# Second mixer of a two-layer trunk: group norm and output projection on half the tokens at a time, in two lanes beside the chain

## The chip, the cores and the metric

One core of one Trainium2 chip. The metric is the device time of one execution in microseconds. A core has engines that run their own queues in order: PE (matrix products; its weight loads are listed as PEld), DVE (elementwise work), ACT (functions and copies), POOL, and SP, which issues nearly all transfers here.

## The reference, cut to what matters

Two layers run over 1104 tokens (16 learned + 1024 prompt tokens, and 64 of a second request), 1024 channels, in f32. The second layer's mixer is RWKV-7: a recurrence over time for each of 16 heads of 64 channels, then

```python
y = moveaxis(scan(step, S0, ...))                # per token and head
y = ((y - mean) * rsqrt(var + GN_EPS)) * ln_w + ln_b   # group norm per head
y = y + bonus                                    # sum(r*k*r_k) * v
y = (y * gate) @ w_o                             # output projection
h = h + y
```

The layer's feed-forward network follows. The kernel computes the recurrence in chunks of 64 tokens.

## The kernel before

`rwkv_a` makes the inputs of the recurrence and leaves them in DRAM: among them the bonus `BV` (stored at L1454) and the gate `GT` (L1156), each as 8 blocks of 128 channels by 1152 tokens. `rwkv_b` runs the recurrence. Channels lie on partitions and tokens along the rows of a tile.

The work is cut into six batches `i`, each a group `g` of 384 tokens (three groups; the first has 320 live tokens) and a half `hf` of the channels (four blocks `ff` of 128). Batch `i` is run in stage `i`, 0 to 5, by `chain`: six chunks of 64 tokens, one after the other, each a row of small matmuls (L1689, L1699, L1704, L1711, L1725) with short steps between them: copies `pm` (L1691), scaled copies (L1705 on ACT, L1706 on DVE), the new state `st` (L1713, L1717), and at the end of a chunk the copy `ysb` of its output (L1726). Beside the chain of batch `i` the stage prepares the next batches: `Bx.build` (tile products, with mask multiplies at L1557 and L1558 on DVE), `Bx.grams`, and `Bx.inverse`, whose start is a substitution of many small DVE operations (L602, L604), then DVE transposes (L618, L620), then small matmuls.

The finished batch `i-1` goes through `tail` in the same stage. First, for each `ff`, it loads `lbv` and `lgt`, squares `y`, sums it with a plain f32 matmul against `bd64` (L1746), takes the inverse root (L1748, L1749 on ACT), and scales, adds and gates on DVE (L1750 to L1752). `split` then makes a rounded part `yh` (ACT, L108) and a remainder `yl` (DVE, L109). Second, for four pairs `mp` of output blocks, `wunit` loads 512 KB of w_o (`raw`), splits it into `wh` (ACT) and `wl` (DVE), and `mm3` sends three products per channel block through PE (L129 to L131). The residual add (L1768, `xt`) follows. In groups 0 and 1 the residual row `xt` is loaded from DRAM and stored again.

What sets the order: each part is a generator, `weave` steps the generators of a stage in turn (each by its share of steps: the chain 36, `tail` 16), and then a scheduler of the framework orders each engine's instructions by that priority and by its own estimate of when inputs are ready. The orders below are what came out. A tile pool with `bufs` slots per tag makes a writer wait until the oldest slot is read; in stages 1 to 4 `raw` has two slots, `wh` and `wl` have one.

Of the kernel before, what the change touches and what calls it, by code (L numbers as in the profile page):

```python
# [51 lines left out]
def tile_trunk(ctx, tc, *aps, stages=("gdn", "ffn0", "rwkv", "ffn1"), dbg=None):  # L52
# [1077 lines left out]
    def gates(tp, xp, dr):  # L1130
# [52 lines left out]
    def rwkv_a(hnp, col, prm, pc, plb, dr, esb, esx, esg, pend, esP):  # L1183
        C = math.exp(-0.5)
        with ExitStack() as es0, ExitStack() as es:
# [246 lines left out]
            with ExitStack() as es, ExitStack() as es1:  # L1432
# [5 lines left out]
                def post_v(ps, n, g, f):  # L1438
# [182 lines left out]
    def rwkv_b(xT, rc, col, plb, dr, Bx, gts, esx, esg, esf, esh, F, more):  # L1621
# [9 lines left out]
        with ExitStack() as esw, ExitStack() as es, ExitStack() as est:  # L1631
# [97 lines left out]
            def tail(g, hf, B):  # L1729
# [5 lines left out]
                for ff in range(4):  # L1735
                    f = 4 * hf + ff
                    bv = tp.tile([P, 384], F32, tag="lbv", bufs=lb, name=uid("lbv"))
                    nc.sync.dma_start(bv[:, :n], dr["BV"][f, :, cs])
                    gt = tp.tile([P, 384], F32, tag="lgt", bufs=lb, name=uid("lgt"))
                    nc.sync.dma_start(gt[:, :n], dr["GT"][f, :, cs])  # L1740
                    y = B["y"][:, ff].rearrange("p c t -> p (c t)")[:, o:]
# [8 lines left out]
                    nc.vector.scalar_tensor_tensor(rs, y, col("rwkv_ln_w", f), rs, ALU.mult, ALU.mult)  # L1750
                    nc.vector.scalar_tensor_tensor(rs, rs, col("rwkv_ln_b", f), bv[:, :n], ALU.add, ALU.add)
                    nc.vector.tensor_tensor(rs, rs, gt[:, :n], ALU.mult)  # L1752
                    split(yy[0][:, ff, :n], yy[1][:, ff, :n], rs)
                    yield
                c0 = LIVE[g][0]
                for mp in range(4):
                    u = wunit(w_o[512 * hf:512 * hf + 512, 256 * mp:256 * mp + 256].rearrange("(k p) c -> p k c", p=P), *wpo)
                    wv = [t.rearrange("p (k m) c -> p k m c", m=2) for t in u]
                    for mm in range(2):
# [21 lines left out]
            tpt, wpo = [], []  # L1781
            ypool = (tp, 2)
            for i, (g, hf) in enumerate(seq):
                Bi = Bx.at(i)
                extra = []
                if i == 5:
# [11 lines left out]
                    if more:  # L1798
                        extra = [(FA, then(first(fp0, hp), F.std(range(N5), (0,), fp0, wunits, lambda i: psB()), F.norms(fp0, (1,))), FO)]
                gens = [(CH, then(chain(i, g, hf, Bi, 0), chain(i, g, hf, Bi, 1)))] + extra  # L1800
                if i == 0:
# [15 lines left out]
                done = tail(g, hf, Bi)  # L1817
            est.close()
# [124 lines left out]
    if "rwkv" in stages:  # L1943
        rs_ = {k: dp_.tile([8, P, 1152], F32, name="r" + k) for k in ("V", "GT", "BV", "R")}
        for k in ("KR", "BK"):
# [50 lines left out]
```

## Time and profile before

| | us |
|---|---|
| median of 3 runs | 3335.11 |
| lowest, highest | 3333.39, 3340.08 |
| the profiled execution | 3338.0 |
| its span | 3336.3 |
| stage 0 of the second mixer's chain ends | 2147.5 |
| stage 5 ends | 2536 |

Times inside the trace are microseconds from the span's start. A stage is taken to end with the sixth `ysb` copy (L1726, on ACT) of its batch, and a chunk with its own. "Busy" is time in which an engine has an instruction; on PE the ends are modelled, since matmuls overlap. The granted clock is the share of full TensorE speed.

### The profile page before, as it was taken

The page shows a single profiled execution, that of the slowest core. Times are in us where ns is not written, and L with a number is a line of the kernel's source. Part 1 is how long each engine was busy: PE and PEld are TensorE (multiplying, and loading weights), DVE is VectorE, ACT ScalarE, POOL GpSimd, SP SyncE. Part 2 cuts the span into 40 slices and gives each one's busy share as a digit, 9 for nine tenths or more (in the row PEclk, how much of TensorE's full clock was granted, in tenths as well). Part 3 has the DMA queues.
Part 4 walks back from the last instruction along what each step waited for, and adds up shares of the span by engine and source line. Part 5 has one row for each costly group of instructions (what it writes and reads, how often), then busy time and mean ns, then how long its engine had stood idle before and what let it go on. Part 6 is the DMA issues. An engine that isn't in the chain of part 4 may idle for free. (4 is left out here: it accounts for less than half of the span.)

```text
span 3336.3 us, 72764 instructions
## 1 busy us (share of the span) xinstructions
PE 3162.9 (95%) x29202; PEld 2974.1 (89%) x29202; DVE 2432.8 (73%) x4835; ACT 1562.6 (47%) x3141; POOL 142.1 (4%) x236
## 2 busy tenths in 40 slices
PE   7999999898999999999999888998989999999998
PEld 6888888797999999999988777777778999999998
DVE  6967768457777667776978863777767687877775
ACT  5876766444433333212777742544445443333112
POOL 1000000002200000000001100000000310000000
PEclk8999999999999999999999899998889999999999
DMA  5433332784332224432255877555556333335231
GB/s 161 120 105 102 100 92 71 268 304 132 99 104 81 79 72 159 130 106 76 78 183 168 278 222 241 148 165 168 152 172 186 100 104 91 94 97 174 88 96 61
DMA packets 543923, 452.69 MB, mean 136 GB/s; under 512 B 78377, under 2 KB 494930, under 8 KB 543458
## 3 DMA queue, kind: packets, MB, share of 16 engines
q1 hardware_dynamic: 538682, 445.61, 43.7%
q8 instruction: 230, 3.77, 0.5%
q10 hardware_dynamic: 4904, 2.43, 0.3%
q14 instruction: 107, 0.88, 0.1%
HBM read 306.86 MB, written 141.07 MB: 134 GB/s over the span
## 5 line engine op out<-in xcount | busy, mean ns | idle before, releaser
L310 PE MATMUL psA<-tc,sh 128*128 128x276 f32 (+1 forms) x1712 | 499.6, 292 | 18.8 <-ACT sh L108 8.2
L312 PE MATMUL psA<-tc,sl 128*128 128x276 f32 (+1 forms) x1712 | 498.9, 291 | 4.0 <-DVE sl L109 3.9
L311 PE MATMUL psA<-tc,sh 128*128 128x276 f32 (+1 forms) x1712 | 498.9, 291 | 0.3 <-DVE tc L109 0.3
L406 DVE TENSOR_TENSOR xT<-xT,psA 128x384 f32<-128x384 f32 (+3 forms) x496 | 252.3, 519 | 136.1 <-PE psA L131 134.4
L310 PEld LDWEIGHTS psA<-tc,sh 128*128 128x128 f32 x1712 | 326.2, 191 | 21.4 <-ACT sh L108 8.6
L108 ACT CAST wh<-raw 128x1024 fp32r<-128x1024 f32 x159 | 166.0, 1047 | 372.5 <-PE psA L130 258.6
L312 PEld LDWEIGHTS psA<-tc,sl 128*128 128x128 f32 x1712 | 325.7, 190 | 5.0 <-DVE sl L109 4.7
L311 PEld LDWEIGHTS psA<-tc,sh 128*128 128x128 f32 x1712 | 325.9, 190 | 1.2 <-DVE tc L109 0.7
L130 PE MATMUL psA<-hl,wh 128*128 128x384 f32 (+3 forms) x1024 | 326.4, 319 | 0.0
L129 PE MATMUL psA<-hh,wh 128*128 128x384 f32 (+3 forms) x1024 | 325.8, 320 | 0.0
L131 PE MATMUL psA<-hh,wl 128*128 128x384 f32 (+3 forms) x1024 | 325.3, 318 | 0.0
L129 PE MATMUL psA<-hnh,wh 128*128 128x384 f32 (+1 forms) x768 | 269.1, 350 | 5.1 <-ACT hnh L108 3.8
L130 PE MATMUL psA<-hnl,wh 128*128 128x384 f32 (+1 forms) x768 | 261.4, 340 | 1.7 <-DVE hnl L109 1.7
L131 PE MATMUL psA<-hnh,wl 128*128 128x384 f32 (+1 forms) x768 | 260.1, 339 | 0.0
L109 DVE TENSOR_TENSOR wl<-raw,wh 128x1024 fp32r<-128x1024 f32 x159 | 195.0, 1228 | 72.8 <-ACT wh L108 72.6
L108 ACT CAST sh<-raw 128x512 fp32r<-128x512 f32 x202 | 124.4, 619 | 251.6 <-PE psA L311 230.8
L129 PE MATMUL psA<-mxh,wh 128*128 128x384 f32 (+1 forms) x672 | 226.4, 348 | 8.3 <-ACT mxh L108 5.3
L130 PE MATMUL psA<-mxl,wh 128*128 128x384 f32 (+1 forms) x672 | 229.2, 343 | 3.6 <-DVE mxl L109 3.5
L131 PE MATMUL psA<-mxh,wl 128*128 128x384 f32 (+1 forms) x672 | 227.5, 340 | 0.3 <-DVE wl L109 0.2
L129 PEld LDWEIGHTS psA<-hh,wh 128*128 128x128 f32 x1024 | 192.0, 188 | 0.7 <-ACT hh L108 0.4
L130 PEld LDWEIGHTS psA<-hl,wh 128*128 128x128 f32 x1024 | 192.3, 188 | 0.3
L131 PEld LDWEIGHTS psA<-hh,wl 128*128 128x128 f32 x1024 | 192.5, 188 | 0.1
(482 smaller groups left out, 7958.8 us busy)
## 6 DMA issues: line engine op xcount, KB each, us to landing
raw<-in_ffn_w_gate_dram SPq DMA_DIRECT2D x64, 512.0 KB
raw<-in_ffn_w_up_dram SPq DMA_DIRECT2D x64, 512.0 KB
raw<-in_ffn_w_down_dram SPq DMA_DIRECT2D x44, 512.0 KB
raw<-in_gdn_w_in_dram SPq DMA_DIRECT2D x32, 512.0 KB
raw<-in_gdn_w_out_dram SPq DMA_DIRECT2D x24, 512.0 KB
raw<-in_rwkv_w_o_dram SPq DMA_DIRECT2D x24, 512.0 KB
hr<-dhid SPq DMA_DIRECT2D x44, 276.0 KB
hr<-dhid SPq DMA_DIRECT2D x44, 272.0 KB
```

Source lines behind the costliest of these rows:

```text
L108: nc.scalar.copy(h, src)
L109: (eng or nc.vector).tensor_tensor(l, src, h.bitcast(F32), ALU.subtract)
L129: nc.tensor.matmul(ps, w[0][:, k, :], x[0][:, k, :n], start=a, stop=False)
L130: nc.tensor.matmul(ps, w[0][:, k, :], x[1][:, k, :n], start=False, stop=False)
L131: nc.tensor.matmul(ps, w[1][:, k, :], x[0][:, k, :n], start=False, stop=z)
L310: nc.tensor.matmul(ps, u[0][:, kk], h, start=first and kk == 0, stop=False)
L311: nc.tensor.matmul(ps, u[0][:, kk], l, start=False, stop=False)
L312: nc.tensor.matmul(ps, u[1][:, kk], h, start=False, stop=last and kk == 3)
L406: nc.vector.tensor_tensor(xT[:, m, a:a + n], xT[:, m, a:a + n], pd[:, :n], ALU.add)
```

## The change

`BV` and `GT` are put into one DRAM tensor `BG`, so that one load `lbg` brings both. `tail` is kept for batches 4 and 5. For batches 0 to 3 it is replaced by two generators that each work on one half (192 columns) of a batch: `normed` (group norm) and `project` (w_o and residual add). The first half of the first group has 128 live columns.

- Stage `i` from 1 to 4 has a lane of `normed`: the second half of batch `i-1`, and (`i` below 4) the first half of batch `i` itself, as soon as `over` says that the chain's first three chunks are issued. Stage 1 begins with the first half of batch 0.
- Its other lane is `project` on batch `i-1`, first half, then second half. It yields until its half is in `ready`.
- `project` loads and splits all of w_o's part again for each half. Two output blocks share one PSUM tile, one residual load, one add and one store; the store is issued a step later (`late`).

The core of the diff:

```diff
-                    bv = tp.tile([P, 384], F32, tag="lbv", bufs=lb, name=uid("lbv"))
-                    nc.sync.dma_start(bv[:, :n], dr["BV"][f, :, cs])
-                    gt = tp.tile([P, 384], F32, tag="lgt", bufs=lb, name=uid("lgt"))
-                    nc.sync.dma_start(gt[:, :n], dr["GT"][f, :, cs])
+                    bg = tp.tile([P, 2, 384], F32, tag="lbg", bufs=lb, name=uid("lbg"))
+                    nc.sync.dma_start(bg[:, :, :n], dr["BG"][:, f, :, cs].rearrange("a p c -> p a c"))
...
+            def window(g, half):
+                o = 384 - LIVE[g][1]
+                lo = max(o, 192 * half)
+                return lo, 192 * half + 192 - lo, LIVE[g][0] + lo - o
...
+            def normed(i, half, out):
...
+                yy = [tp.tile([P, 4, 192], F32R, tag=t, bufs=2, name=uid(t)) for t in ("yh", "yl")]
+                for ff in range(4):
...
+                    ps = psC()
+                    nc.tensor.matmul(ps[:, :n], bd64, rs, start=True, stop=True)
+                    nc.scalar.activation(rs, ps[:, :n], AF.Ln, bias=gne)
+                    nc.scalar.activation(rs, rs, AF.Exp, scale=-0.5)
+                    nc.vector.scalar_tensor_tensor(rs, yf, col("rwkv_ln_w", f), rs, ALU.mult, ALU.mult)
+                    nc.vector.scalar_tensor_tensor(rs, rs, col("rwkv_ln_b", f), bg[:, 0, :n], ALU.add, ALU.add)
+                    nc.vector.tensor_tensor(rs, rs, bg[:, 1, :n], ALU.mult)
+                    split(yy[0][:, ff, :n], yy[1][:, ff, :n], rs)
+                    yield
+                out[i, half] = yy
...
+            def project(i, half, out):
+                while (i, half) not in out:
+                    yield
...
+                for mp in range(4):
+                    u = wunit(w_o[512 * hf:512 * hf + 512, 256 * mp:256 * mp + 256].rearrange("(k p) c -> p k c", p=P))
...
+                    nc.sync.dma_start(xt, X)
+                    ps = psC()[:, :2 * n].rearrange("p (m n) -> p m n", m=2)
+                    for mm in range(2):
+                        mm3(ps[:, mm], (wv[0][:, :, mm], wv[1][:, :, mm]), yy, range(4), n)
+                        if mm:
+                            nc.vector.tensor_tensor(xt, xt, ps, ALU.add)
+                        elif late:
+                            nc.sync.dma_start(*late)
+                        yield
+                    late = X, xt
...
+                    lane = [normed(0, 0, ready)] if i == 1 else []
+                    lane.append(normed(i - 1, 1, ready))
+                    if i < 4:
+                        lane.append(after(i, normed(i, 0, ready), over))
+                    gens.append((8 * max(len(lane), 2), then(*lane)))
+                    gens.append((TA, then(project(i - 1, 0, ready), project(i - 1, 1, ready))))
                 weave(*gens)
```

The order of instructions is the same before stage 1 and after stage 5. Within, two places are shown.

DVE, near the end of its queue before the first `st` of stage 3 (before, that is four rows further on). `wl` is a weight remainder, `mb` and `kb` are mask multiplies of `build`, `b32u` and `b32t` belong to the substitution, `xT` from `psA` is the chain's scaled copy. Before:

```order
L602 TENSOR_TENSOR b32u<-b32a,b32t 128x120
L1557 TENSOR_TENSOR mb<-psB,rmk 64x192
L1558 TENSOR_TENSOR kb<-psB,rmk 64x3x2x64
L1557 TENSOR_TENSOR mb<-psB,rmk 64x192
L1558 TENSOR_TENSOR kb<-psB,rmk 64x3x2x64
L604 TENSOR_TENSOR b32t<-b32t,b32u 128x2x10x6
L602 TENSOR_TENSOR b32u<-b32a,b32t 128x126
L604 TENSOR_TENSOR b32t<-b32t,b32u 128x2x9x7
L602 TENSOR_TENSOR b32u<-b32a,b32t 128x128
L1706 TENSOR_SCALAR xT<-psA 64x260
```

After, at the same place (`yl` is the remainder of a normed half, `xt` the residual add):

```order
L1819 TENSOR_TENSOR xt<-xt,psC 128x384
L109 TENSOR_TENSOR wl<-raw,wh 128x1024
L1557 TENSOR_TENSOR mb<-psB,rmk 64x192
L1558 TENSOR_TENSOR kb<-psB,rmk 64x3x2x64
L1557 TENSOR_TENSOR mb<-psB,rmk 64x192
L1558 TENSOR_TENSOR kb<-psB,rmk 64x3x2x64
L1706 TENSOR_SCALAR xT<-psA 64x260
L1794 SCALAR_TENSOR_TENSOR gsq<-ysb,prm,gsq 128x192
L1795 SCALAR_TENSOR_TENSOR gsq<-gsq,prm,lbg 128x192
L1796 TENSOR_TENSOR gsq<-gsq,lbg 128x192
L109 TENSOR_TENSOR yl<-gsq,yh 128x192
L1819 TENSOR_TENSOR xt<-xt,psC 128x384
```

The substitution, which stood around the chain's copy, now ends further ahead, with its transposes, as the next piece shows; a half norm and an add stand between the copy and the next `st`.

DVE again, after, in the middle of the same queue, some twenty rows further ahead:

```order
L604 TENSOR_TENSOR b32t<-b32t,b32u 128x2x15
L618 STREAM_TRANSPOSE b32tnh<-b32t 128x16x32
L620 STREAM_TRANSPOSE b32tt<-b32t 128x32x32
L1557 TENSOR_TENSOR mb<-psB,rmk 64x192
L1558 TENSOR_TENSOR kb<-psB,rmk 64x3x2x64
L1557 TENSOR_TENSOR mb<-psB,rmk 64x192
L1558 TENSOR_TENSOR kb<-psB,rmk 64x3x2x64
L1794 SCALAR_TENSOR_TENSOR gsq<-ysb,prm,gsq 128x192
L1795 SCALAR_TENSOR_TENSOR gsq<-gsq,prm,lbg 128x192
L1796 TENSOR_TENSOR gsq<-gsq,lbg 128x192
L109 TENSOR_TENSOR yl<-gsq,yh 128x192
```

Before, these two transposes stood in the fourth chunk of the stage.

PE, the end of its queue before the chain's products L1711 of the same chunk. Before:

```order
L1699 MATMUL psA<-xT 64x64 x8
L1563 MATMUL psB<-ident,bk 128x128 x3
L1704 MATMUL psA<-pm,ttf 64x65 x8
L1746 MATMUL psC<-gsq,bd 128x384
L1711 MATMUL psA<-xT 64x65
L1569 MATMUL psB<-rcx,V 64x65 x4
L1711 MATMUL psA<-xT 64x65 x7
```

After:

```order
L1704 MATMUL psA<-pm,ttf 64x65 x8
L1791 MATMUL psC<-gsq,bd 128x192
L129 MATMUL psC<-yh,wh 128x192
L130 MATMUL psC<-yl,wh 128x192
L131 MATMUL psC<-yh,wl 128x192
L129 MATMUL psC<-yh,wh 128x192
L130 MATMUL psC<-yl,wh 128x192
L131 MATMUL psC<-yh,wl 128x192
L129 MATMUL psC<-yh,wh 128x192
L130 MATMUL psC<-yl,wh 128x192
L131 MATMUL psC<-yh,wl 128x192
```

Projection matmuls of 192 columns now stand between the chain's products L1704 and L1711; the chunk holds 60 of them, where it held 36 of 320.

More of the change, by code (lines that the diff above doesn't have):

```diff
@@ new lines, in project @@
+            def project(i, half, out):
+                while (i, half) not in out:
+                    yield
+                yy = out.pop((i, half))
+                g, hf = seq[i]
+                _, n, c0 = window(g, half)
+                tp = tpt[0]
+                late = None
+                for mp in range(4):
+                    u = wunit(w_o[512 * hf:512 * hf + 512, 256 * mp:256 * mp + 256].rearrange("(k p) c -> p k c", p=P))
+                    wv = [t.rearrange("p (k m) c -> p k m c", m=2) for t in u]
+                    X = dr["X"][:, 2 * mp:2 * mp + 2, c0:c0 + n]
+                    xt = tp.tile([P, 2, 192], F32, tag="xt", bufs=3, name=uid("xt"))[:, :, :n]
+                    nc.sync.dma_start(xt, X)
[6 more added lines that the diff above has]
+                            nc.sync.dma_start(*late)
+                        yield
+                    late = X, xt
+                nc.sync.dma_start(*late)
@@ L1773, in first, with after, flagged @@
+            def after(key, gen, flags):
+                while key not in flags:
+                    yield
+                yield from gen
+            def flagged(gen, key, flags):
+                yield from gen
+                flags.add(key)
             def first(tp, hp):
@@ L1781, in rwkv_b @@
             tpt, wpo = [], []
+            ready, over = {}, set()
             ypool = (tp, 2)
@@ L1799, in rwkv_b @@
                         extra = [(FA, then(first(fp0, hp), F.std(range(N5), (0,), fp0, wunits, lambda i: psB()), F.norms(fp0, (1,))), FO)]
-                gens = [(CH, then(chain(i, g, hf, Bi, 0), chain(i, g, hf, Bi, 1)))] + extra
+                gens = [(CH, then(flagged(chain(i, g, hf, Bi, 0), i, over), chain(i, g, hf, Bi, 1)))] + extra
                 if i == 0:
@@ L1809, in rwkv_b @@
                     gens.append((GA, gts, GO))
-                else:
-                    gens.append((TA, done))
+                elif i == 5:
+                    gens.append((TA, done))
+                else:
+                    lane = [normed(0, 0, ready)] if i == 1 else []
[4 more added lines that the diff above has]
+                    gens.append((TA, then(project(i - 1, 0, ready), project(i - 1, 1, ready))))
                 weave(*gens)
@@ L1816, in rwkv_b @@
                     tpt[:] = pool(est, "rt", 2), 2, cb
-                done = tail(g, hf, Bi)
+                if i > 3:
+                    done = tail(g, hf, Bi)
             est.close()
@@ L1943, in tile_trunk @@
     if "rwkv" in stages:
-        rs_ = {k: dp_.tile([8, P, 1152], F32, name="r" + k) for k in ("V", "GT", "BV", "R")}
-        for k in ("KR", "BK"):
+        rs_ = {k: dp_.tile([8, P, 1152], F32, name="r" + k) for k in ("V", "R")}
+        for k in ("KR", "BK", "BG"):
             rs_[k] = dp_.tile([2, 8, P, 1152], F32, name="r" + k)
```

18 lines of the change are left out of this document (14 added, 4 removed).

## The prediction

> **What bounds the kernel now.** I read the page first, then the busy times stage by stage. The page gives span and TensorE.
>
> ```profile
> span 3336.3 us, 72764 instructions
> PE 3162.9 (95%) x29202; PEld 2974.1 (89%) x29202; DVE 2432.8 (73%) x4835; ACT 1562.6 (47%) x3141; POOL 142.1 (4%) x236
> ```
>
> The order of instructions differs only in stages 1 to 5 of the second mixer's chain, 2147.5 to 2536 us. A stage ends with its sixth `ysb` copy. Next, busy times of these stages; columns: span, then PE, PEld, DVE, ACT, POOL, granted clock, DMA share, GB/s.
>
> ```profile
> 2147.50:2220.50 73.00, 67.20 (x1580) 56.11 (x1579) 56.80 (x131) 37.22 (x86) 1.84 (x4) 0.91 0.59 166
> 2220.50:2301.50 81.00, 69.98 (x1570) 59.28 (x1570) 59.35 (x137) 35.49 (x80) 1.84 (x4) 0.85 0.58 164
> 2301.50:2379.40 77.90, 71.33 (x1569) 60.25 (x1569) 60.85 (x138) 36.38 (x79) 1.84 (x4) 0.89 0.56 155
> 2379.40:2459.00 79.60, 71.27 (x1507) 60.21 (x1506) 61.58 (x144) 33.65 (x76) 0.85 (x4) 0.89 0.45 127
> 2459.00:2536.00 77.00, 70.51 (x819) 59.99 (x819) 53.99 (x98) 38.27 (x76) 0.00 (x0) 0.96 0.63 199
> ```
>
> PE idles 6 to 11 us a stage and DVE 16 to 23. The average hides two regimes, which the six chunks of stage 3 (between `ysb` copies) show; the last two rows are the first chunks of stages 2 and 4.
>
> ```profile
> 2301.40:2319.50 18.10, 16.17 (x258) 13.31 (x256) 16.12 (x44) 8.30 (x19) 0.00 (x0) 1.00 0.65 178
> 2319.50:2327.00 7.50, 6.99 (x148) 5.48 (x146) 7.08 (x19) 4.54 (x12) 0.00 (x0) 1.00 0.66 176
> 2327.00:2337.30 10.30, 6.82 (x123) 5.06 (x121) 9.87 (x27) 4.59 (x13) 0.00 (x0) 1.00 0.70 202
> 2337.30:2357.90 20.60, 19.95 (x557) 17.04 (x557) 14.34 (x28) 6.92 (x15) 1.53 (x3) 0.59 0.46 122
> 2357.90:2367.30 9.40, 9.40 (x214) 8.57 (x211) 5.21 (x11) 4.04 (x9) 0.00 (x0) 1.00 0.42 125
> 2367.30:2379.40 12.10, 12.10 (x293) 10.90 (x287) 8.33 (x14) 8.06 (x16) 0.31 (x1) 1.00 0.53 148
> ...
> 2220.40:2236.90 16.50, 15.43 (x258) 12.91 (x256) 15.70 (x46) 7.38 (x18) 0.00 (x0) 1.00 0.65 183
> ...
> 2379.40:2398.10 18.70, 17.40 (x234) 14.86 (x232) 16.31 (x45) 7.90 (x18) 0.00 (x0) 0.91 0.67 186
> ```
>
> Chunks 1 to 3 are DVE's (87 to 96% busy), chunks 4 to 6 PE's (97 to 100%), chunk 4 at a granted clock of 0.59.
>
> **The change: work added.** Each projected batch loads and splits w_o twice, so stages 1 to 4 get 4 units more each, 16 in all. Each norm step works on 192 columns instead of 384, in twice as many instructions. The rows that price this on DVE and ACT:
>
> ```profile
> L109 DVE TENSOR_TENSOR wl<-raw,wh 128x1024 fp32r<-128x1024 f32 x15 | 18.3, 1222 | 7.6 <-ACT wh L108 7.5
> L108 ACT CAST wh<-raw 128x1024 fp32r<-128x1024 f32 x15 | 15.7, 1046 | 32.4 <-DMA raw<-in_rwkv_w_o_dram 11.7 <-PE psC L130 10.8 <-DVE b32u L602 7.6
> L1750 DVE SCALAR_TENSOR_TENSOR gsq<-ysb,prm,gsq 128x384 f32<-128x384 f32 x8 | 4.9, 612 | 3.3 <-ACT gsq L1749 3.3
> L1750 DVE SCALAR_TENSOR_TENSOR gsq<-ysb,prm,gsq 128x320 f32<-128x320 f32 x8 | 4.4, 549 | 1.2 <-ACT gsq L1749 1.1
> L1752 DVE TENSOR_TENSOR gsq<-gsq,lgt 128x384 f32<-128x384 f32 x8 | 4.4, 552 | 0.1
> L1752 DVE TENSOR_TENSOR gsq<-gsq,lgt 128x320 f32<-128x320 f32 x8 | 3.9, 483 | 0.1
> ```
>
> DVE: 16 x 1.22 = 20 us for the weights. A norm op costs 1.0 ns a column by its two forms: 0.42 us (L1750, and L1751 like it) or 0.35 us (L1752, and the `yl` remainder like it) at 192 columns, 1.54 us for the four against 2.32 at 384; two halves of 16 f: 16 x 0.76 = 12 us. DVE gets 32 us more; it was busy for 0.70 to 0.78 of these stages. ACT: 16 x 1.05 = 17 us and about as much for the norm as DVE; at 45% busy I cost it at nothing. Its wait for single-buffered weights comes 16 times oftener (10.8 us in 9 waits now), with the chain's `pm` and `ysb` copies queued behind it; were that not hidden, 19 us, within the range.
>
> PE: 192 matmuls for a batch instead of 96. Next, their pitch at full clock, at half clock, then weight loads whose matmuls have only 64 columns.
>
> ```profile
> 3200.43 0.33 PE L131 MATMUL psA<-hh,wl 128*128 128x384 f32 x1
> 3200.60 0.34 PE L129 MATMUL psA<-hh,wh 128*128 128x384 f32 x1
> ...
> 2387.03 0.53 PE L131 MATMUL psC<-yh,wl 128*128 128x384 f32 x1
> 2387.35 0.53 PE L129 MATMUL psC<-yh,wh 128*128 128x384 f32 x1
> ...
> 765.81 0.30 PEld L1051 LDWEIGHTS psB<-QG,S 128*128 128x128 f32 x2
> 766.03 0.30 PEld L1052 LDWEIGHTS psB<-QG,gss 128*128 128x128 f32 x2
> 766.26 0.30 PEld L1049 LDWEIGHTS psB<-QK,vn 128*128 128x128 f32 x2
> ```
>
> A 384-column matmul takes 0.17 us (0.32 at half clock); a weight load takes 0.112 us even where its matmul is short. No row shows this kind of matmul under 256 columns. Below, half of 0.17, 0.09 us; above, a plain f32 matmul of 192 columns: 0.34 us (rival B). I take 0.112, since the weights change with every matmul: 768 x 0.112 = 86 us, against 192 x 0.17 + 192 x 0.145 (320 columns, by the same slope) = 60: PE gets 26 us more. The Trainium skill (TensorE: Matmul & The Clock Gate, Back-to-back issue gap) gives an isolated matmul N/2.4 + 2.5 ns, 83 ns for 192 columns and 56 for the 192 matmuls of 128, by which PE would get 2 us less; the 64-column rows above, at twice that, speak against it.
>
> SP: one load stands for two norm operands, in 768-byte rows; loads and stores of x keep their number. The 16 more loads of 512 KB are 8.4 MB, 52 us at 162 GB/s, beside a DMA share below 0.6. ACT waited 11.7 us in 3 of 15 units for such a load; 16 more cost 0 to 12 us, and I take 0, since the load now stands earlier.
>
> **Where it lies.** The first chunk of stages 2 to 4 decides, since DVE is full there and works in order. By the order, DVE's queue between the last `st` of a stage and the first of the next (I call it the hump) held in stage 3:
>
> - before: 12 mask multiplies (L1557, L1558), 18 substitution ops (L602, L604), 2 weight remainders, 3 residual adds, 5 chain ops;
> - after: the same, but 24 substitution ops, and both transposes (L618, L620) and 12 half-norm ops as well.
>
> ```profile
> L1558 DVE TENSOR_TENSOR kb<-psB,rmk 64x384 f32<-64x384 f32 x46 | 25.5, 555 | 0.8
> L1557 DVE TENSOR_TENSOR mb<-psB,rmk 64x192 f32<-64x192 f32 x46 | 16.1, 350 | 1.3 <-PE psB L1554 0.8
> L604 DVE TENSOR_TENSOR b32t<-b32t,b32u 128x30 f32<-128x30 f32 (+7 forms) x60 | 15.0, 250 | 1.2
> L1768 DVE TENSOR_TENSOR xt<-xt,psC 128x320 f32<-128x320 f32 (+1 forms) x29 | 14.9, 515 | 22.7 <-PE psC L131 21.2 <-DMA bk<-rBK 1.3
> L620 DVE STREAM_TRANSPOSE b32tt<-b32t 128x1024 f32<-128x1024 f32 x4 | 7.6, 1899 | 0.0
> L618 DVE STREAM_TRANSPOSE b32tnh<-b32t 128x512 f32<-128x512 f32 x4 | 4.3, 1082 | 0.0
> L1713 DVE TENSOR_TENSOR st<-psA,plb 128x260 f32<-128x260 f32 x24 | 10.1, 422 | 3.9 <-PE psA L1711 2.9
> ```
>
> Before: 6 x 0.555 + 6 x 0.35 + 18 x 0.25 + 2 x 1.22 + 3 x 0.515 + 1.8 (chain: two copies taken at 0.28, three ops at 0.42) = 15.7 us. After: 1.5 more for substitution, 3.0 for transposes, 3 x 1.54 = 4.6 for norms: 24.8. Stage 4 has the same two lists. Stage 2 goes from 16.0 to 29.5, with 30 substitution ops, four remainders and five adds. Elapsed over queue was 18.1/15.7, 16.5/16.0 and 18.7/15.7, mean 1.12; so 28, 33 and 28 us, that is +16.5, +10 and +9: **+35.5 us**. With nothing lost between ops it is 29.5 + 2 x 24.8 - 53.3 = +26.
>
> The other chunks go by the longer queue. Stage 3: chunk 2 gains two remainders (DVE 8.9 against 7.5 elapsed, +1.4); chunk 3 loses its substitution (DVE 7.7), but PE takes 34 projection matmuls, 3.8 us (-1); chunk 4 has 24 x 0.112 instead of 12 at half clock, 0.32 (-1); chunks 5 and 6 become DVE's at 10.3 and 13.0 (+1, +1). Net +1. Likewise +5 in stage 1 (norm and projection in one chunk), 0 in stage 2, -3 in stage 4, -6 in stage 5 (norm and the first matmuls thinner): **-3 us**.
>
> The sum is +33. The profiled run took 3338.0 us (span 3336.3), 2.9 above the median of 3335.11. 3338 + 33 - 3 = 3368 us.
>
> **The rivals.**
>
> A, the forecast: DVE's hump decides; +10 to +55, 3345 to 3390. Chance 0.55.
>
> B, short matmuls run at the plain f32 rate. For it: the kernel has no such matmul under 256 columns. Against: the rate per column is steady from 384 down to 256. The plain rate, two records a matmul:
>
> ```profile
> L1059 PE MATMUL psC<-sq,ones 128*128 128x512 f32 x36 | 19.1, 613 | 0.6 <-ACT sq L1056 0.6
> L1054 PE MATMUL psB<-QG,S 128*128 128x128 f32 x112 | 21.7, 275 | 0.0
> ```
>
> (613 - 275)/384 = 0.88 ns a column, 1.76 for two: 0.34 us at 192 columns, 0.225 at 128. PE gets 576 x 0.23 + 192 x 0.113 = 154 us on top; about 40 hide under DVE's hump: 3368 + 114, about 3480. Chance 0.25, by the missing rows alone.
>
> C, faster: the projection now runs from the start of a stage and keeps PE fed, so that chunk 4 (20.6 us at clock 0.59) runs at full clock, and DVE works off part of the hump in chunks 4 to 6, where it idled 14 us of 42. It decides if the first chunk stays under some 20 us. Then chunk 4 loses 4 to 6 us in three stages and stage 5 its 6: 3335 - 21 = 3314. The Trainium skill (same page, Part 1) has the clock at 4/8 after an idle window of about 3.4 us, and full again after a busy one; the 0.32 us pitch agrees with a half clock, and an earlier projection would help by this rule. Against C: the hump is in order, ahead of the chain's op. Chance 0.10.
>
> D, no change: humps at +26 less C's 21, or any such balance: within 7 us of 3335. Chance 0.10.
>
> **How the numbers follow.** The likeliest is A: 3368. The range must leave out no more than 0.2: it goes from 3330 (D in, C out) to 3480 (half of B); A's own is 3345 to 3390. About 0.2% (7 us) is what a measurement can tell from no change. Faster 0.10, same 0.10, slower 0.80.
>
> **What would show it.** Right: first chunks of stages 2 to 4 of 27 to 33 us with DVE above 85%; 16 more `wl` at 1.22 us; a 192-column pitch near 0.11 us. Wrong: a pitch of 0.3 us (B); first chunks under 20 us with chunk 4 at full clock (C).

## The result, and the profile after

The changed kernel takes 3437.55 us (median of 4 runs, 3436.58 to 3444.93) beside 3334.25 (4 runs, 3330.55 to 3340.08) for the kernel before: a ratio of 1.031, 95% interval 1.0297 to 1.0323. That is +103 us, where +33 was forecast. The first two lines of the page:

```profile
span 3435.7 us, 73801 instructions
PE 3230.9 (94%) x29618; PEld 3045.0 (89%) x29618; DVE 2465.2 (72%) x4915; ACT 1589.8 (46%) x3221; POOL 142.5 (4%) x236
```

Next, the busy times of stages 1 to 5, with the columns of the prediction's table.

```profile
2147.68:2226.94 79.26, 72.27 (x1615) 62.37 (x1615) 60.69 (x150) 42.06 (x109) 1.84 (x4) 0.85 0.60 170
2226.94:2338.17 111.23, 92.47 (x1745) 82.80 (x1745) 75.59 (x173) 46.83 (x107) 1.84 (x4) 0.88 0.55 158
2338.17:2447.24 109.07, 90.47 (x1673) 79.88 (x1674) 67.60 (x153) 43.38 (x100) 1.84 (x4) 0.78 0.44 122
2447.24:2553.06 105.82, 89.22 (x1605) 78.43 (x1606) 67.44 (x155) 36.99 (x86) 0.85 (x4) 0.74 0.39 112
2553.06:2631.51 78.45, 68.58 (x819) 58.15 (x819) 53.33 (x97) 38.40 (x77) 0.00 (x0) 0.93 0.62 192
```

Stages 2 to 4 took 81.0, 77.9 and 79.6 us, and now take 111.2, 109.1 and 105.8: nearly all of the loss. No engine is full: PE is busy for 83 to 84% of them, DVE for 62 to 68%. Now the first four chunks of stage 3, then first chunk and second and third together, of stages 2 and 4.

```profile
2338.17:2367.76 29.59, 22.48 (x267) 19.50 (x267) 24.16 (x63) 11.76 (x28) 0.42 (x1) 0.82 0.51 142
2367.76:2382.81 15.05, 11.98 (x170) 10.44 (x170) 8.67 (x19) 4.95 (x13) 0.00 (x0) 0.78 0.60 169
2382.81:2398.67 15.86, 14.43 (x174) 12.51 (x177) 8.87 (x20) 4.23 (x10) 0.00 (x0) 0.72 0.46 133
2398.67:2422.20 23.53, 19.19 (x569) 17.35 (x563) 10.64 (x23) 7.65 (x16) 1.11 (x2) 0.65 0.32 89
...
2226.90:2265.00 38.10, 30.08 (x329) 26.81 (x329) 28.47 (x75) 13.63 (x33) 0.42 (x1) 0.87 0.61 176
2265.00:2293.00 28.00, 24.59 (x360) 21.95 (x354) 19.41 (x43) 11.18 (x28) 0.00 (x0) 0.90 0.62 181
...
2447.20:2481.40 34.20, 25.18 (x242) 21.55 (x243) 26.62 (x69) 11.25 (x27) 0.85 (x4) 0.65 0.48 137
2481.40:2512.80 31.40, 27.12 (x320) 23.23 (x323) 17.42 (x38) 8.79 (x23) 0.00 (x0) 0.73 0.37 106
```

The second and third chunks of stages 2 and 4 before:

```profile
2236.50:2259.10 22.60, 15.28 (x288) 11.73 (x280) 16.93 (x44) 9.48 (x24) 0.00 (x0) 0.85 0.67 191
...
2397.70:2413.90 16.20, 14.38 (x266) 10.41 (x258) 15.43 (x41) 8.16 (x21) 0.00 (x0) 1.00 0.60 170
```

First chunks take 38.1, 29.6 and 34.2 us, where 33, 28 and 28 were forecast. The second and third together take 28.0, 30.9 and 31.4 us, where they took 22.6, 17.8 and 16.2; the forecast had them nearly unchanged. Here PE is busy for 80 to 91% and DVE for 55 to 69%, and neither queue is full.

The price of the added work is as forecast. Half-norm operations of 192 columns take 0.415 us on DVE (L1794, 24 of them). The DVE group of the weight remainders in stages 1 to 4, then PE rows of stage 3 at full clock and behind a wait (start, duration):

```profile
L109 DVE TENSOR_TENSOR wl<-raw,wh 128x1024 fp32r<-128x1024 f32 x31 | 37.9, 1223 | 12.3 <-ACT wh L108 11.6
```

```profile
2338.99 0.27 PE L131 MATMUL psC<-yh,wl 128*128 128x192 f32 x1
2339.10 0.28 PE L129 MATMUL psC<-yh,wh 128*128 128x192 f32 x1
...
2344.95 0.36 PE L129 MATMUL psC<-yh,wh 128*128 128x192 f32 x1 [3.34 <-DMA lbg<-rBG]
...
2347.24 0.41 PE L129 MATMUL psC<-yh,wh 128*128 128x192 f32 x1
2347.46 0.41 PE L130 MATMUL psC<-yl,wh 128*128 128x192 f32 x1
```

192 columns start 0.11 us apart, as taken, and 0.22 soon after TensorE had stood for 3.34 us. So what grew is waiting, and time at half clock. Some of the waits in stages 1 to 4, after (us in total, times, longest):

```profile
ACT yh L108 <- DVE gsq L1796: 55.8, 27, 6.3
ACT pm L1691 <- PE psA L1689: 28.4, 14, 5.4
DVE st L1713 <- PE psA L1711: 18.9, 15, 2.2
```

and before:

```profile
ACT pm L1691 <- PE psA L1689: 15.3, 13, 4.0
ACT yh L108 <- DVE gsq L1752: 9.0, 9, 1.9
DVE st L1713 <- PE psA L1711: 2.9, 5, 1.4
```

ACT stands for DVE in the norm six times as long, and both chain steps in the list wait longer for PE.

### The profile page after: what moved, and what is told of

It reads as the page before. It is cut to its first block, busy times and chain, and to the rows that moved or that the text cites. A ratio compares the mean times of both kernels' runs of the same rounds, so it can differ in the third digit from the quotient of the medians.

```text
span 3435.7 us, 73801 instructions
## 1 busy us (share of the span) xinstructions
PE 3230.9 (94%) x29618; PEld 3045.0 (89%) x29618; DVE 2465.2 (72%) x4915; ACT 1589.8 (46%) x3221; POOL 142.5 (4%) x236
## 5 line engine op out<-in xcount | busy, mean ns | idle before, releaser
L310 PE MATMUL psA<-tc,sh 128*128 128x276 f32 (+1 forms) x1712 | 501.0, 293 | 18.6 <-ACT sh L108 7.7
L108 ACT CAST wh<-raw 128x1024 fp32r<-128x1024 f32 x175 | 182.5, 1045 | 354.4 <-PE psA L130 260.2
L129 PE MATMUL psA<-hh,wh 128*128 128x384 f32 (+3 forms) x1024 | 326.0, 320 | 0.0
L131 PE MATMUL psA<-hh,wl 128*128 128x384 f32 (+3 forms) x1024 | 325.7, 318 | 0.0
L129 PE MATMUL psA<-hnh,wh 128*128 128x384 f32 (+1 forms) x768 | 269.4, 351 | 5.3 <-ACT hnh L108 4.1
L109 DVE TENSOR_TENSOR wl<-raw,wh 128x1024 fp32r<-128x1024 f32 x175 | 214.7, 1228 | 79.2 <-ACT wh L108 78.3
L131 PE MATMUL psA<-hnh,wl 128*128 128x384 f32 (+1 forms) x768 | 260.5, 339 | 0.0
L129 PE MATMUL psA<-mxh,wh 128*128 128x384 f32 (+1 forms) x672 | 226.1, 347 | 7.9 <-ACT mxh L108 4.6
L131 PE MATMUL psA<-mxh,wl 128*128 128x384 f32 (+1 forms) x672 | 227.4, 340 | 0.2 <-DVE wl L109 0.2
L129 PEld LDWEIGHTS psA<-hh,wh 128*128 128x128 f32 x1024 | 192.2, 188 | 0.8 <-ACT hh L108 0.6
L131 PEld LDWEIGHTS psA<-hh,wl 128*128 128x128 f32 x1024 | 192.7, 188 | 0.1
```

What stands on the lines that cost most here:

```text
L108: nc.scalar.copy(h, src)
L109: (eng or nc.vector).tensor_tensor(l, src, h.bitcast(F32), ALU.subtract)
L129: nc.tensor.matmul(ps, w[0][:, k, :], x[0][:, k, :n], start=a, stop=False)
L131: nc.tensor.matmul(ps, w[1][:, k, :], x[0][:, k, :n], start=False, stop=z)
L310: nc.tensor.matmul(ps, u[0][:, kk], h, start=first and kk == 0, stop=False)
```

## The experiments

Each run is set against runs of the kernel before on the same chip; the medians of that kernel lay between 3334 and 3344 us, so the column "us more" is the fair one.

| kernel | us | us more than before | ratio, 95% interval |
|---|---|---|---|
| before, 16 units reloaded | 3345.56 | +9.9 | 1.0027 (1.0015 to 1.0040) |
| before, matmuls in column halves | 3395.99 | +60.3 | 1.0176 (1.0159 to 1.0192) |
| before, two overlapping 256-column pieces | 3353.27 | +17.6 | 1.0047 (1.0032 to 1.0061) |
| before, norm in halves | 3332.94 | -2.8 | 0.9985 (0.9975 to 0.9995) |
| after, padded to 256 columns | 3353.51 | +18.6 | 1.0047 (1.0032 to 1.0061) |
| after, padded to 254 columns | 3439.37 | +95.0 | 1.0284 (1.0256 to 1.0312) |
| after, two slots for wh and wl | 3440.25 | +105.4 | 1.0299 (1.0274 to 1.0324) |
| after, one unit for both halves | 3411.00 | +76.1 | 1.0214 (1.0189 to 1.0238) |
| the same, padded to 256 | 3388.54 | +44.2 | 1.0118 (1.0080 to 1.0157) |
| after, five lbg tiles | 3437.79 | +102.9 | 1.0300 (1.0279 to 1.0321) |

**The parts alone.** The theory from the prediction was that DVE's queue in the first chunk decides (order theory); its rivals were the doubled units with their relay from load to ACT, DVE and TensorE (weights theory) and the short matmuls' time on TensorE (matmul theory). First the reload alone:

```diff
+                        if mm and g < 2:
+                            u = wunit(w_o[512 * hf:512 * hf + 512, 256 * mp:256 * mp + 256].rearrange("(k p) c -> p k c", p=P), *wpo)
+                            wv = [t.rearrange("p (k m) c -> p k m c", m=2) for t in u]
```

> The kernel before, with each unit of the output matrix loaded and split a second time for the second output block of its pair, for the first four batches: 16 more loads, 16 more wh copies on ACT and 16 more wl subtractions on DVE, as in the changed kernel, while norm and matmuls stay whole. In its DVE order the first chunks keep 16 to 17 us of queue, so they do not grow by the order. Order theory (the growth comes from what the order puts into the first chunks): at most the subtractions themselves, 16 x 1.22 = 20 us, and since chunks 4 to 6 wait for TensorE rather about 5: 3335 to 3355. Weights theory (every added unit is a relay load, ACT, DVE, TensorE that the in-order queues make wait, in the changed trace 16 us before L129's matmuls and 8 us before L131's): 3365 to 3420. Matmul theory: no change, 3335 to 3340.

+9.9 us: 16 units more are a tenth of the loss, less than their 20 us of DVE. The weights theory, in this size, falls.

The matmuls alone, in halves of 192 and then in pieces of 256:

```diff
+                        for a, b in ((0, n - 192), (n - 192, n)):
+                            mm3(ps[:, a:b], w2, [t[:, :, a:b] for t in yy], range(4), b - a)
```

> The kernel before, with every projection matmul of the first four batches issued as two column halves of at most 192, the weights loaded once and the norm whole. TensorE gets 192 x 0.11 us pitch in place of 96 x 0.17 per batch, worked out for the prediction as +26 us in all. The first chunks' DVE queue is 18 us in place of 16. Matmul theory: chunks 4 to 6, where TensorE is the longer queue, take the whole +26, 3350 to 3362. Order theory: 6 us by the first chunks and little more, 3335 to 3345. Weights theory: no change, 3335 to 3340.

```diff
-                            for a, b in ((0, n - 192), (n - 192, n)):
+                            for a, b in ((0, 256), (n - 256, n)):
```

> As the kernel with column halves of 192, but the two pieces overlap and are 256 columns wide each, which TensorE takes at nearly the same pitch but which the order places otherwise: first chunks of 22.3, 22.3 and 20.6 us of DVE queue in stages 2 to 4 in place of 18.0, 18.0 and 17.0. The overlapping columns are written twice with the same values. Order theory: 12 us above the kernel with halves of 192. Matmul theory: within 5 us of it (a pitch of 0.12 in place of 0.11 would give 384 x 2 x 0.01 = 8 at the very most). Weights theory: the same as before.

All three theories miss: halves of 192 cost 60 us, the wider pieces, with a longer DVE queue in the first chunk, only 18. In the kernel with halves of 192, rows of DVE, PE and ACT in the first chunk of stage 2, with the busy times of the stretch between the last two:

```profile
2235.25 1.86 DVE L620 STREAM_TRANSPOSE b32tt<-b32t 128x1024 f32<-128x1024 f32 x1
2237.37 1.19 DVE L109 TENSOR_TENSOR wl<-raw,wh 128x1024 fp32r<-128x1024 f32 x1
...
2238.61 0.48 PE L131 MATMUL psC<-yh,wl 128*128 128x128 f32 x1 [6.55 <-DVE wl L109]
...
2238.60:2249.40 10.80, 10.79 (x52) 10.29 (x53) 2.22 (x5) 0.00 (x0) 0.00 (x0) 0.50 0.42 123
...
2249.44 1.04 ACT L108 CAST wh<-raw 128x1024 fp32r<-128x1024 f32 x1 [18.93 <-PE psC L130]
```

The order put `wl` behind the whole substitution and its transposes. TensorE, in order, stood 6.55 us for it; its matmuls then ran at half clock (0.50) for 10.8 us; ACT stood 18.93 us to write the next `wh`, whose single slot those matmuls held, and the chain's copies stood behind that. The first chunk took 34.9 us with 18 us of DVE queue. So a queue's length is not its cost: the places in it are.

The norm alone in halves:

```diff
-                    y = B["y"][:, ff].rearrange("p c t -> p (c t)")[:, o:]
-                    rs = tp.tile([P, 384], F32, tag="gsq", bufs=1, name=uid("gsq"))
+                    for p0, p1 in ((o, 384),) if g == 2 else ((o, 192), (192, 384)):
```

> The kernel before, with the group norm of the first four batches done on two column halves one after the other (the loads, the units of the output matrix and the projection stay whole): twice the instructions of the norm, DVE +12 us, ACT +17 us as in the prediction's terms. By its DVE order the first chunks of stages 2 to 4 hold 24.7, 23.6 and 26.4 us in place of 16.2, 15.8 and 16.0, the next chunk 3 to 5 us more. Order theory: these stand in the path, +27 to +38 us, 3360 to 3375, of which the changed kernel's humps (+49) would be two thirds. Weights theory and matmul theory: the 12 us of DVE at most, 3335 to 3347.

Not slower at all. Its first chunk of stage 2, and the last three of that stage:

```profile
2201.60:2224.80 23.20, 21.30 (x282) 18.20 (x282) 20.91 (x57) 9.99 (x25) 0.00 (x0) 1.00 0.68 203
...
2243.00:2276.00 33.00, 28.08 (x994) 24.27 (x987) 23.52 (x57) 20.78 (x52) 1.43 (x3) 0.95 0.54 153
```

The first chunk grew to 23.2 us, as its DVE queue said, but the last three fell from 41.9 (81.0 less 16.5 and 22.6) to 33.0, so the stage is shorter (74.4 us, before 81.0). In sum stages 1 to 5 took 387.5 us (before 388.5): stages 1 to 3 were shorter, and stage 5 took 90.3 (before 77.0). The order theory as the prediction had it falls here: a longer hump moved work about and cost nothing in the end.

**The order, not TensorE.** The decisive pair pads the halves and makes the matmuls 256 and then 254 columns wide.

```diff
-                yy = [tp.tile([P, 4, 192], F32R, tag=t, bufs=2, name=uid(t)) for t in ("yh", "yl")]
+                yy = [tp.tile([P, 4, 256], F32R, tag=t, bufs=2, name=uid(t)) for t in ("yh", "yl")]
+                for z in yy:
+                    nc.gpsimd.memset(z[:, :, n:256].bitcast(F32), 0.0)
```

> The changed kernel with the halves of yh and yl padded to 256 columns (the padding zero, written by POOL) and the projection's matmuls 256 columns wide in place of 192; all else as in the changed kernel. The DVE order then holds 24.7, 21.0 and 20.2 us in the first chunks of stages 2 to 4 in place of 29.8, 25.4 and 25.4. Order theory: 15 us faster than the changed kernel, 3422. Weights theory: the same as the changed kernel, 3437. Matmul theory: not faster, 3437 to 3450.

```diff
-                        mm3(ps[:, mm], (wv[0][:, :, mm], wv[1][:, :, mm]), yy, range(4), 256)
+                        mm3(ps[:, mm], (wv[0][:, :, mm], wv[1][:, :, mm]), yy, range(4), 254)
```

> The kernel with the halves padded to 256 columns and matmuls of 256 (3353.5, 84 us faster than the changed kernel), with 254 columns in place of 256: two columns less for TensorE, and the order falls back to one like the changed kernel's (first chunks of 30.4, 24.1 and 24.1 us of DVE queue in stages 2 to 4, in place of 24.7, 21.0 and 20.2). In the traces the matmuls of 192 and of 256 columns start 0.11 and 0.12 us apart at full clock. Order theory (the static order is what 192 columns change, TensorE itself gains nothing from 256): the 84 us come back, 3420 to 3445, with a pitch of 0.11 to 0.12 still. Width theory (the padding itself, or something that TensorE does better at wide matmuls, brought the 84): 3350 to 3360. Weights theory: as at 256, 3350 to 3360.

256 columns take back 85 of the 103 us, far more than any theory had; 254 lose 76 of them again, as the order theory had it. The matmuls' pitch in the two kernels, 256 first:

```profile
2310.84 0.28 PE L130 MATMUL psC<-yl,wh 128*128 128x256 f32 x1
2310.95 0.28 PE L131 MATMUL psC<-yh,wl 128*128 128x256 f32 x1
```

```profile
2347.86 0.28 PE L131 MATMUL psC<-yh,wl 128*128 128x254 f32 x1
2347.98 0.28 PE L129 MATMUL psC<-yh,wh 128*128 128x254 f32 x1
```

Both 0.11 to 0.12 us: TensorE sees no step between them. What differs is the order of the queues: of DVE's 627 entries in stages 1 to 4, 92% stand in the same sequence at 192 as at 254 columns, and 60% at 254 as at 256. The order is worth 76 to 85 us. That the scheduler prices such matmuls much dearer below 256 columns is the likely reason; the runs show the step in the order, not its price. One place where it costs time can be read on ACT and PE in the second chunk of stage 3; first the changed kernel:

```profile
2376.32 0.35 ACT L108 CAST yh<-gsq 128x192 fp32r<-128x192 f32 x1 [1.33 <-DVE gsq L1796]
2377.10 0.36 ACT L1788 ACTIVATE gsq<-ysb 128x192 f32<-128x192 f32 x1 [0.42 <-DVE yl L109]
2377.37 1.03 ACT L108 CAST wh<-raw 128x1024 fp32r<-128x1024 f32 x1
2378.30 0.38 ACT L1705 ACTIVATE xT<-psA 64x260 f32<-64x260 f32 x1
...
2378.73 0.33 PE L1711 MATMUL psA<-xT 128*64 128x65 f32 x2 [2.54 <-ACT xT L1705]
```

and the kernel with 256 columns:

```profile
2335.42 1.04 ACT L108 CAST wh<-raw 128x1024 fp32r<-128x1024 f32 x1 [0.44 <-PE psC L130]
2336.38 0.38 ACT L1705 ACTIVATE xT<-psA 64x260 f32<-64x260 f32 x1
...
2336.80 0.33 PE L1711 MATMUL psA<-xT 128*64 128x65 f32 x2 [0.34 <-ACT xT L1705]
...
2337.12 0.35 ACT L108 CAST yh<-gsq 128x192 fp32r<-128x192 f32 x1
```

In the changed kernel the half norm's `yh`, which waits for three DVE operations, and the next Square stand ahead of the chain's L1705. In the other L1705 comes first and `yh` finds its operand ready. PE stands 2.54 us for L1705 there, and 0.34 at 256 columns. In all of stages 1 to 4 it stood 5.2 us for L1705 (0.8 at 256), so this meeting alone is a small part of the loss. The wait of `yh` in stages 1 to 4 is 55.8 us at 192 columns; at 254 and at 256 it is:

```profile
ACT yh L108 <- DVE gsq L1798: 53.6, 27, 6.3
```

```profile
ACT yh L108 <- DVE gsq L1798: 12.4, 9, 3.2
```

The half clock goes with the loss too. Stages 1 to 4 at 256 columns:

```profile
2140.02:2217.76 77.74, 70.11 (x1615) 60.22 (x1614) 60.58 (x151) 41.78 (x108) 3.34 (x8) 0.89 0.59 165
2217.76:2310.09 92.33, 86.52 (x1745) 76.44 (x1746) 70.98 (x168) 46.58 (x108) 3.96 (x10) 0.94 0.63 181
2310.09:2389.99 79.90, 74.53 (x1673) 65.85 (x1674) 67.40 (x159) 43.43 (x99) 3.12 (x8) 0.96 0.63 180
2389.99:2470.36 80.37, 73.75 (x1605) 65.01 (x1606) 65.18 (x154) 37.18 (x86) 1.57 (x6) 0.94 0.53 151
```

They have the changed kernel's matmuls in number, wider ones, but PE is busy for 304.9 us of 330.3 at a granted 0.89 to 0.96, against 344.4 of 405.4 at 0.74 to 0.88. So of the 75.1 us between the two, 39.5 are PE's work at a lower clock and 35.5 its standing idle.

**Slots and loads.** Two slots for wh and wl, one unit for both halves, and more lbg tiles:

```diff
-                    set_wp(est, 2, 1)
+                    set_wp(est, 2, 2)
```

> The changed kernel with two slots each for wh and wl in stages 1 to 4 in place of one (and two xt tiles in place of three, to make room). Weights theory in its first form (a unit's split waits for the matmuls of the unit before, since each slot is single): the 16 us before L129 and the 8 us before L131 go, 3400 to 3415. Weights theory in its second form (the split waits in the queues of ACT and DVE behind other work): about the same, 3430 to 3440. Order theory: first chunks of 33.0, 25.4 and 25.4 us, 3 us more than the changed kernel, 3438 to 3443. Queue theory (the SP queue is held by loads that wait for a slot): the same as the changed kernel or some us slower for the lost xt tile.

No gain: not the slots. The waits did go: PE stood 1.2 us before L129 and 1.2 before L131, where it had stood 15.7 and 8.0, and the time stayed.

```diff
-            def project(i, half, out):
-                while (i, half) not in out:
+            def project(i, out):
+                while (i, 0) not in out or (i, 1) not in out:
...
+                    for half in range(2):
+                        yy = out[i, half]
```

> The changed kernel with each unit of the output matrix loaded and split once for both halves: the projection waits until both halves are normed, and the first half of the next batch is normed only after that. 16 loads, 16 wh copies and 16 wl subtractions less than the changed kernel; norm in halves and matmuls of 192 columns stay. First chunks by the DVE order: 28.0, 28.1 and 29.2 us, 4 us more in sum than the changed kernel, and 32 TensorE-side waits for units become 16. Weights theory: it takes back the 24 us of waits and the 20 us of DVE, 3385 to 3405. Order theory: the first chunks stay, 3425 to 3445. Matmul theory: no change, 3430 to 3440.

27 us less than the changed kernel, between the ranges of the weights and the order theory, though its first chunks of stages 2 and 3 took 47.2 and 50.7 us. With both edits:

> The changed kernel with each unit loaded once for both halves and with the halves padded to 256 columns: what is left of the change are the norm in halves and the lane's place. Alone the reload cost 9.9 us in the kernel before, and the padding left 19 of the 103. Sum of parts: 3353.5 - 9.9 = 3344. If the first chunk's queue rules, it is slower than that: its order holds 27.3, 30.2 and 29.4 us in the first chunks, with 132 to 168 projection matmuls ahead of the chain's there in place of 36: 3375 to 3410.

+44.2, slower than the padding alone (+18.6): the parts don't add. Waiting for both halves puts 132 to 168 projection matmuls ahead of the chain's in the first chunk, which is the likely reason; the time lies in the range of the first chunk's queue.

```diff
-                    bg = tp.tile([P, 2, 192], F32, tag="lbg", bufs=3, name=uid("lbg"))
+                    bg = tp.tile([P, 2, 192], F32, tag="lbg", bufs=5, name=uid("lbg"))
```

> The changed kernel with five lbg tiles in place of three (and two xt tiles in place of three, to make room); the orders of all the engines are the changed kernel's. In the changed trace the SP queue stood 48 us before L1785's loads, waiting for a lbg tile, and the loads for the builds queued behind. Queue theory: 10 to 30 us faster than the changed kernel, 3407 to 3427. Order, weights and matmul theories: the same as the changed kernel, 3432 to 3442.

The same time, but the run hardly took the wait away: SP stood 39.0 us in 6 waits for L1796 before L1785's loads, where it had stood 48.2 in 11. At 256 columns this wait is gone, and at 254 it is 41.4 us, so it comes and goes with the loss. Against it as the cause: in stages 1 to 4 of the changed kernel the waits of PE, DVE and ACT that the trace puts down to a transfer come to 9.2 us (before, 19.6). SP's queue is unlikely, then, but the run doesn't exclude it.

**Which place in the order.** Four suspects were left: (a) a unit's `wl` behind the substitution in DVE's queue, (b) the mere length of that queue in the first chunk, (c) the projection's matmuls ahead of the chain's on TensorE, (d) `yh` on ACT ahead of the chain's copies. For (a), each product of the substitution is queued behind the last `wl`.

```diff
+            with tc.issue_after(lastwl[0]) if pinned[0] and lastwl else ExitStack():
+                nc.vector.tensor_tensor(wv, a[:, :, j + 1:, j:j + 1].to_broadcast([P, 2, m, c]),
```

| kernel | us | us more than before | ratio, 95% interval |
|---|---|---|---|
| column halves, wl ahead | 3374.41 | +31.1 | 1.0093 (1.0059 to 1.0127) |
| after, wl ahead | 3434.40 | +91.1 | 1.0268 (1.0223 to 1.0313) |
| before, wl ahead | 3343.73 | +0.4 | 1.0000 (0.9985 to 1.0016) |
| norm in halves, wl ahead | 3346.88 | +3.6 | 1.0008 (0.9992 to 1.0024) |
| after, yh on DVE | 3444.90 | +103.8 | 1.0316 (1.0274 to 1.0357) |
| the same, wl ahead | 3427.83 | +86.7 | 1.0254 (1.0226 to 1.0283) |
| the same, four gsq tiles | 3411.98 | +75.3 | 1.0225 (1.0202 to 1.0247) |
| before, norm in halves for three batches | 3337.12 | -7.2 | 0.9979 (0.9962 to 0.9996) |

> The kernel with whole norm, weights once and matmuls in column halves (60 us slower than before), with one thing more: in stages 1 to 4 each product of the substitution is queued on DVE behind the wl last asked for, so that the wl stands ahead of the substitution. The number of projection matmuls in each chunk is unchanged (72 in the first chunk, 24, 48, 48 in the last three). There the first chunks took 34.9, 35.9 and 33.4 us, of which TensorE stood 6.5 for the wl and ACT 18.9 behind a wh copy; the DVE queue in them was only 18. Theory (a), the wl behind the substitution is the stall: the first chunks fall to the 22 us of DVE queue that the new order holds, 11 to 13 us in each of three: 3355 to 3365. Theory (b), the length of DVE's queue: 22.3 in place of 18.0, so 13 us slower, 3405 to 3410. Theory (c), the matmuls ahead of the chain's: no change, 3390 to 3400.

29 of its 60 us go: in that kernel the suspect was half of it. The first chunks took 27.6, 26.6 and 25.6 us.

> The changed kernel with the substitution queued behind the last wl in the same way; its projection matmuls stay where they were in TensorE's queue (110, 49, 33 in the first three chunks of stage 2). DVE's first chunks hold 19.2, 19.3 and 19.3 us in place of 29.8, 25.4 and 25.4, the second ones 19.8, 13.5 and 13.5 in place of 12.1, 8.9 and 8.9. Theory (a): most of the 103 goes, 3360 to 3385. Theory (b): 22 us less in the first chunks and 17 more in the second, 3425 to 3435. Theory (c): 3430 to 3440.

12 of 103, with overlapping intervals: in the changed kernel (a) is a small part at most. The time lies in the ranges of (b) and (c); but with 19 us of DVE queue the first chunks still took 30.2, 28.4 and 28.4 us, so that queue alone doesn't fill them. The two controls, the second also a candidate:

> Control: the kernel before with the substitution queued behind the last wl. Its order has the first wl at a place where TensorE waited only 0.8 us for it, and the first chunks hold 16.4, 15.9 and 16.1 us in place of 16.2, 15.8 and 16.0. All theories: the same as before within 10 us, 3325 to 3345.

> The kernel before with the norm in halves for four batches (2.8 us faster than before) and the substitution queued behind the last wl. First chunks by DVE's queue: 18.7, 18.1 and 18.8 us in place of 24.7, 23.6 and 26.4, the second ones 14.8 to 15.6 in place of 11.7 to 14.0. Theory (a): that kernel waits little for wl, so the gain is small: 3320 to 3333. Theory (b): 15 us off the first chunks, 7 on the second: 3320 to 3327. It is the candidate for a version that beats both.

Where the `wl` was in time, the move brings nothing; and with the norm in halves, first chunks with 5 to 8 us less of DVE queue gained nothing (+3.6 us where the halves alone had -2.8, the intervals just overlapping), which speaks against (b). For (d), the `yh` copy was put on DVE:

```diff
-                    split(yy[0][:, ff, :n], yy[1][:, ff, :n], rs)
+                    nc.vector.tensor_copy(yy[0][:, ff, :n], rs)
+                    nc.vector.tensor_tensor(yy[1][:, ff, :n], rs, yy[0][:, ff, :n].bitcast(F32), ALU.subtract)
```

> The changed kernel with the yh copy of the half norms on DVE in place of ACT, behind the product that it copies, so that ACT no longer waits there and the chain's copies are not queued behind that wait. DVE gets 32 copies of up to 192 columns more, about 0.3 us each, 10 us; its first chunks hold 34.7, 26.6 and 26.6 us in place of 29.8, 25.4 and 25.4. The projection's matmuls stand in TensorE's chunks nearly as before (132, 27, 33 in stage 2, 60, 26, 34 in stage 3). Theory (d), ACT's wait is on the path: of the 47 us that this wait grew, most goes: 3390 to 3410, with the second and third chunks of stages 2 to 4 at 9 to 11 us in place of 15 to 16. Theory (c), the matmuls: 3435 to 3450. DVE's queue alone: 7 us slower, 3445.

No gain, as (c) and the length of DVE's queue both had it. But the wait was not taken away: it moved to the next instruction on ACT, the Square, whose tile DVE frees:

```profile
ACT gsq L1788 <- DVE yl L1798: 56.9, 25, 6.8
```

> The same, and the substitution queued on DVE behind the last wl: both suspected waits, ACT for DVE in the norm and TensorE for the wl behind the substitution, are taken away, at 10 us more of DVE and with 32 units and matmuls of 192 columns still. First chunks by DVE's queue 27.3, 20.5 and 20.5 us. Theories (a) and (d) together: 3365 to 3390, nearer to the kernel with 256 columns (3353). Theory (c): 3430 to 3445.

17 us less than with `yh` on DVE alone (the intervals just overlapping), far from the range of (a) and (d) together. So the last run gave the Square two more tiles (`bufs=2` to `bufs=4`):

> The changed kernel with the yh copy on DVE and the substitution behind the last wl (3427.8), with four gsq tiles in place of two, so that the Square on ACT no longer waits for DVE's yl (there 49.6 us, 23 times, with wh and the chain's copies queued behind). Orders and places else the same: first chunks by DVE's queue 27.3, 20.5 and 20.5 us. Theory (d): 25 to 45 us faster, 3383 to 3403, and the second and third chunks of stages 2 to 4 fall from 14 to 16 us towards 11. Theory (c): within 8 us of it, 3420 to 3436.

11 us less than with two tiles, between the ranges of (d) and (c), the intervals just overlapping. Its wait, and its second and third chunk of stage 3:

```profile
ACT gsq L1795 <- DVE yl L1805: 25.6, 13, 4.8
```

```profile
2348.51:2363.60 15.09, 10.93 (x171) 9.49 (x170) 14.11 (x39) 4.35 (x12) 0.00 (x0) 0.89 0.58 162
2363.60:2378.93 15.33, 14.22 (x174) 12.36 (x177) 11.98 (x24) 3.97 (x9) 0.42 (x1) 0.72 0.50 141
```

The wait halved (from 49.6 us), but these chunks still take 15 us, one now with DVE nearly full and one with PE busy at 0.72 of its clock; what was gained lies in other chunks. All moves together bring 28 of the 103 us, beyond the intervals. No single place that was tried holds the rest; (c) wasn't tried by itself, and what speaks against it alone is that the first three chunks of stages 3 and 4 hold about as many projection matmuls in the order at 256 columns as at 192.

**A version that beats both.** Norm in halves for the first three batches only, all else as before:

```diff
-                    for p0, p1 in ((o, 384),) if g == 2 else ((o, 192), (192, 384)):
+                    for p0, p1 in ((o, 192), (192, 384)) if 2 * g + hf < 3 else ((o, 384),):
```

> The kernel before with the norm in halves for the first three batches only (two gsq tiles of half the size, a tag of their own). With halves for four batches stages 1 to 3 were 7, 7 and 3 us shorter than before, and stage 5 was 13 us longer. If the halves themselves gain in a stage: 3315 to 3325, faster than the kernel before. If the work that a shorter stage leaves over comes due in a later one in any case: 3328 to 3336.

7 us faster than before, the interval ending just short of 1; on the base that was expected from (3335.7), 3328. Its stages 1 to 3 take 66.1, 74.6 and 75.1 us (before 72.9, 81.0 and 78.0) and stage 4 takes 86.5 (79.5): nearly half of the gain comes due later, as the second expectation has it.

## Why the prediction was wrong

- **What bounds the kernel**: right in part. "DVE is full there" left out PE, which was as busy in the first chunks of stages 2 to 4 (94, 89 and 93%, DVE 95, 89 and 87%).
- **The added work**: right. 16 more `wl` at 1.22 us, half-norm operations of 0.415 us, a pitch of 0.11 us. Rival B falls on TensorE; a step at 256 columns exists, but in the order.
- **"A 384-column matmul takes 0.17 us ... PE gets 26 us more"**: right as a price, and too little for what came. At 256 columns PE was busy for 304.9 us in stages 1 to 4, 25 more than the 279.8 before; in the changed kernel it was 344.4. The other 40 go with the granted clock, 0.78 and 0.74 in stages 3 and 4; at half clock a matmul of 192 columns takes 0.22 us. The forecast's sum let no wait lower the clock. Rival C looked at the clock and had its sign wrong: stage 3 fell from 0.89 to 0.78, and its chunk 4 took 23.5 us at 0.65.
- **"At 45% busy I cost it at nothing"** (ACT): the wrong measure. ACT is busy for 35 to 42% of stages 2 to 4 after, and still stands where the chain's copies are queued behind its waits. The price kept for it, 19 us, was for the weights; the wait that grew (47 us) was the norm's. What that wait cost isn't settled: moving it gained nothing, and halving it on its new place 11 us.
- **The hump**: right in place and sign, +49 us (38.1 - 16.5, 29.6 - 18.1, 34.2 - 18.7) against +35.5. But not by its mechanism, so that the size came near is luck: DVE was 75 to 82% busy in these chunks, under the 85% that the prediction asked for; with the queue cut to 19 us they still took 28 to 30; and the norm in halves shows that a longer DVE queue there is no loss by itself. The forecast counted the queue and not what stood idle behind its entries.
- **"The other chunks go by the longer queue"**: this step failed outright. It gave -3 us; the five stages grew by 95 in all, so outside the humps by 47, of which 34 in the second and third chunks of stages 2 to 4. The rule held in stage 3 before, where each chunk had one full engine; in stage 2 it had failed already (second and third chunk: 22.6 us with PE busy for 15.3 and DVE for 16.9). After, none is full there; in the chunk whose rows are shown, the half norm's steps on ACT and DVE and a unit's `wh` stand in order ahead of the chain's L1705, for which PE waits. How much of the 34 us such places make was not measured.
- **The sum**: stages 1 to 4 grew by 94 us. By PE, with the kernel at 256 columns as the measure, about 25 are the added matmuls' price, 40 its work at a lower clock and 29 its standing idle. By cause, 76 to 85 of the 103 us come with the order that the kernel gets below 256 columns (in the kernel before, short matmuls alone make 60, and 18 at 256). The remaining 18 to 27 are not split further, since the parts don't add: the reload costs 10 us in the kernel before, while loading once, with the wait for both halves, gains 27 in the changed kernel and loses 26 at 256 columns. Which places of that order hold the 76 is settled for 28 us and open beyond: a wait that was taken away came back, in part or whole, on another queue.

## What to carry to other kernels

Where a scheduler fixes the queues when the kernel is built, a change of a tile's width can change the order far from it: price the order too, and try the next width up (here 254 against 256 columns, 76 us) before blaming an engine. Don't price a chunk by the longest queue's length when no engine is full in it; follow, in order, who stands behind each waiting instruction, and ask where the wait goes once it is removed. When a stage shrinks, look at what comes due in the next one.

## What the runs showed of the hardware

Matmuls of 128 rows and columns of weights, with new weights each, start 0.11 us apart at 192 columns, 0.12 at 254 and 256, and 0.17 at 384: from 192 to 256 columns the width hardly matters. The Trainium skill (TensorE: Matmul & The Clock Gate, LDWEIGHTS) has a weight load take its columns over 1.2 ns, 107 ns here, which fits; by its Back-to-back issue gap of N/2.4 + 2.5 ns it would be 83 at 192 columns, which doesn't; the section gives this for an isolated matmul and says itself that it counts too little at few columns. Soon after 3.34 us without work the same matmuls started 0.22 us apart; Part 1 of the same page of the Trainium skill has the clock at half after an idle window of about 3.4 us, and this place agrees. So long a stand wasn't needed everywhere: in the kernel before, the granted clock fell from 1.00 to 0.50 between 2385 and 2386 us, with no stand of PE over 0.77 us in the 5 us ahead. Nor did being busy bring it back at once: with halves of 192, PE worked without a stand for 10.8 us at 0.50.
